# Three elementwise additions of a hybrid encoder kernel made by accumulating DMA transfers

## The chip, the cores and the metric

The kernel runs on one core of a Trainium2 chip. A core has a matrix engine (PE, with its weight loads as PEld), a vector engine (DVE), an activation engine (ACT), a general engine (POOL) and a queue engine (SP), which work side by side and wait for each other by semaphores; 16 DMA engines move data between memory and the core. DMAs are issued from the queues of SP, ACT and POOL. The metric is the device time of one execution in microseconds (us), the median of several; less is better.

## The reference

Two layers over 1040 positions (16 meta tokens ahead of 1024) of width 1024. Each layer has a mixer (a gated delta rule in both directions with 4 heads of 128, beside a short gated convolution) and a SwiGLU feed-forward part, each with an RMS norm ahead of it and added to the residual. Cut to what matters:

```python
def rmsnorm(x, w):
    y = xf * lax.rsqrt(jnp.mean(xf * xf, axis=-1, keepdims=True) + RMS_EPS)
    return y * w

def chunk_gated_delta_rule(q, k, v, g, beta):
    G = jnp.cumsum(g, axis=-1)
    incl = jnp.tril(jnp.ones((CHUNK, CHUNK), dtype=bool))
    decay_mat = jnp.exp(jnp.where(incl, G[..., :, None] - G[..., None, :], -jnp.inf))
    M = jnp.where(strict, jnp.einsum('bnhid,bnhjd->bnhij', kb, k) * decay_mat, 0.0)
    ...                     # triangular solves with I + M, then a scan over the chunks
def swiglu(h, w_gate_up, w_down):
    gate, up = jnp.split(h @ w_gate_up, 2, axis=-1)
    return (jax.nn.silu(gate) * up) @ w_down

for l in range(DEPTH):
    h = h + hybrid_mixer(rmsnorm(h, norm1_w[l]), ...)
    h = h + swiglu(rmsnorm(h, norm2_w[l]), w_gate_up[l], w_down[l])
h = rmsnorm(h, final_norm_w)
```

## The kernel before

Everything lies with channels on the 128 partitions and positions along the row. Matrix products in full precision are made of three passes: weights and inputs are split into a high and a low part (`whi`, `wlo`; `a`, `b` and others), and each tile of 128 channels takes high times high, high times low and low times high (L156 to L158 in `dense`, L1064 to L1066 in `prod`, L1430 to L1432 for the last product). A weight tile is loaded by SP into a `raw` or `ck2` buffer, ACT copies its high part (L129, L1046) and POOL, in some stretches DVE, subtracts for the low part (L130, L1047).

The program is written in Python as a list of instructions, and a planner, which simulates the times of instructions and transfers, draws up each engine's order from priorities and from what it reckons to be ready. On the chip every engine and every queue then goes through its own list strictly in order: an instruction that waits holds all behind it. Buffers with one tag are shared in turn; a new use waits until the old one is over. `after` and `at_prio` write some orders by hand.

A layer goes through these stages. Input projection: tiles of keys (`seq` 4 to 7), queries, values, gates and the convolution's channels. When the keys are there, `normalise` sends their lengths through memory on POOL's queue (`rnd`, L415, and `bc`, L418) and DVE multiplies (L419). `chunk_p` then makes, for each of nine chunks and two directions `d`, the decay matrix: row sums `gd` are loaded to all partitions into one of eight buffers `ptm` (L459, on ACT's queue), DVE adds a mask `off` of 0 and 1e30 (L460), ACT takes the exponential (L462), the result is stored (`dtd`, L463) and DVE multiplies it with the keys' products (L465). `sub_start` reuses the buffers of `ptm`: ACT copies the diagonal blocks (L521), DVE transposes them (L523), `substitute` inverts them on DVE (L533, L535), and `invert` finishes on PE (L544 transposes, L560 first product). For the first chunk, `meta` does small operations on POOL (L478, L479). A scan over the chunks follows (loads at L783 to L789).

Output projection: `out_part(z, m)` makes eight tiles `m` for each of two halves `z` of the positions; DVE adds them to the residual (L909), ACT squares them into `sq`, of which there are two buffers with the tag `c` (L953), and the squares are added to the running sum `ss` (in the profile `rstd`) by DVE, or by POOL for the even tiles of the second half (L954). `finish_bc` makes the norm's factors from the sums (L206 to L214). Beside it DVE and ACT prepare the inputs `T` of the feed-forward part (L177, L968 to L1005).

Feed-forward part: gate and up together are a two by two product of blocks done with seven products instead of eight. For each tile `f` of 22 the weights A11, A12, A21, A22 are loaded, and DVE forms sums and differences of them: `s1t` = A21 + A22 (L1288), `s2t` (L1289, L1292), A11 - A21 (L1293). `w_op` splits each. `NE` = 4: for the first four tiles the products with A11 and A12 are made ahead, under the end of the output projection. The tag `ck2` has five buffers, each `f` takes four of them. The down projection follows in the same way (`w_unit`, `t_pair`).

The lines that the change touches, outside the two functions:

```python
        off = sb.tile([128, 2, 128], F32, tag="off", name=nm("off"))
        dma(off.rearrange("p a b -> p (a b)"), cst_d[:, C_NF:C_NF + 256])          # L325
        ...
            s1t, s2t = raw4("ck2"), raw4("ck2")
            ...
            tt(out=s1t, in0=A21, in1=A22, op=ALU.add)                             # L1288
```

Of the kernel before, what the change touches and what calls it, by code (L numbers as in the profile page):

```python
# [7 lines left out]
F32 = mybir.dt.float32  # L8
# [3 lines left out]
ALU = mybir.AluOpType  # L12
# [6 lines left out]
H = 4  # L19
# [23 lines left out]
def trunk(ctx: ExitStack, tc: tile.TileContext, xT, w_in, w_ba, w_out, w_gu, w_dn,  # L43
          par_d, alog_d, dtb_d, cst_d, eye_d, out):
    nc = tc.nc
    sb = ctx.enter_context(tc.tile_pool(name="sb", bufs=1))
# [5 lines left out]
    def nm(p):  # L52
        cnt[0] += 1
        return f"{p}_{cnt[0]}"
# [220 lines left out]
    dma(alog, alog_d.partition_broadcast(128))  # L275
    dma(dtb, dtb_d.partition_broadcast(128))

    hsrc = xT
    for l in range(DEPTH):
        last = l == DEPTH - 1  # L280
# [39 lines left out]
        hd = dram.tile([KT, 128, L], F32, name=nm("hd"))  # L320
        m0d = dram.tile([2, 2, 4, 16, 16], F32, name=nm("m0d"))
        rsd = [dram.tile([4, 260], F32, name=nm("rsd")) for _ in range(2)]

        off = sb.tile([128, 2, 128], F32, tag="off", name=nm("off"))
        dma(off.rearrange("p a b -> p (a b)"), cst_d[:, C_NF:C_NF + 256])  # L325


        gt = big("P0")
# [117 lines left out]
        def chunk_p(c):  # L446

            if not Pd:
                Pd.extend(sb.tile([128, 4 * L], F32, tag=f"P{d}", name=nm("P")) for d in range(2))
                Pv.extend(p[:, 0:4096].rearrange("p (q i) -> p q i", i=128) for p in Pd)  # L450
                p_ = sb.tile([128, 4 * L], F32, tag=Y[0][2], name=nm("ptm"))
                ptm.extend(p_[:, 512 * i:512 * i + 512].rearrange("p (h i) -> p h i", h=4) for i in range(8))
            n, s0 = span(c)
            kk = bank("b").rearrange("p (h i) -> p h i", h=4)
            for h in range(H):
                mm(kk[0:n, h, 0:n], KTt[:, h, s0:s0 + n], KTt[:, h, s0:s0 + n], start=True, stop=True)
            for d in (dirs0 if c == 0 else (0, 1)):
                gr = ptm[(2 * c + d) % 8]
                adma(gr[0:n, :, 0:n], gd[36 * d + 4 * c:36 * d + 4 * c + 4, 0:n].partition_broadcast(n))  # L459
                tt(out=gr[0:n, :, 0:n], in0=gr[0:n, :, 0:n], in1=off[0:n, d, 0:n].unsqueeze(1).to_broadcast([n, 4, n]), op=ALU.add)  # L460
                for h in range(H):
                    act(out=gr[0:n, h, 0:n], in_=gr[0:n, h, 0:n], func=AF.Exp, scale=-1.0, bias=nGb[0:n, d, c, h:h + 1])  # L462
                adma(dtd[c, d].rearrange("p (h i) -> p h i", h=4)[0:n, :, 0:n], gr[0:n, :, 0:n])  # L463
                dst = P0[d] if c == 0 else Pv[d][:, 4 * c - 4:4 * c, :]
                tt(out=dst, in0=kk[0:n, :, 0:n], in1=gr[0:n, :, 0:n], op=ALU.mult)  # L465
                if c == 0:

                    def meta():
                        mt = t2k("mt").rearrange("p a b -> p (a b)")[0:4].rearrange("p (w a b) -> p w a b", w=2, a=16)
                        Wm, Zm = mt[:, 0], mt[:, 1]  # L470
                        Tm = t2k("mt").rearrange("p a b -> p (a b)")[0:4, 0:256].rearrange("p (a b) -> p a b", a=16)
                        dma(m0d[d, 0].rearrange("h j i -> j h i"), P0[d])
                        dma(Wm, m0d[d, 0])
                        dma(Zm, eye_d[0:4, :, :][:, 0:16, 0:16])
                        for s in (range(15, 0, -1) if d == 0 else range(0, 15)):
                            r0, r1, a0, a1 = (0, s, s, 16) if d == 0 else (s + 1, 16, 0, s + 1)
                            sh = [4, r1 - r0, a1 - a0]
                            ptt(out=Tm[:, r0:r1, a0:a1], in0=Wm[:, r0:r1, s:s + 1].to_broadcast(sh), in1=Zm[:, s:s + 1, a0:a1].to_broadcast(sh), op=ALU.mult)  # L478
                            ptt(out=Zm[:, r0:r1, a0:a1], in0=Zm[:, r0:r1, a0:a1], in1=Tm[:, r0:r1, a0:a1], op=ALU.subtract)  # L479
                        dma(m0d[d, 1], Zm)  # L480
                        dma(P0[d], m0d[d, 1].rearrange("h j i -> j h i"))

                    meta()
# [461 lines left out]
        def out_part(z, m):  # L945
            dense(wload(w_out[l, m, :, 0:4, :], 4), os_, hcut[z], add_h(m), pwide)

            v, sv = half(hr[m][:, o0:L], z), half(ss[:, o0:L], z)
            if m == 0:
                act(out=sv, in_=v, func=AF.Square)  # L950
            else:
                sq = c4k("sq")[:, 0:NB].rearrange("p (g e) -> p g e", g=2)
                act(out=sq, in_=v, func=AF.Square)  # L953
                (ptt if z == 1 and m % 2 == 0 else tt)(out=sv, in0=sv, in1=sq, op=ALU.add)  # L954
            for (n0, n1) in hcut[z]:
                dma(hd[m][:, n0:n1], hr[m][:, n0:n1])

# [320 lines left out]
        for f in range(FT):  # L1278
            A11, A12, A21, A22 = raw4("raw"), raw4("raw"), raw4("ck2"), raw4("ck2")
            dma(A11, w_gu[l, f, 0, :, 0:4, :])  # L1280
            dma(A21, w_gu[l, f, 1, :, 0:4, :])
            dma(A22, w_gu[l, f, 1, :, 4:8, :])
            dma(A12, w_gu[l, f, 0, :, 4:8, :])
            s1t, s2t = raw4("ck2"), raw4("ck2")
            W = {}
            if f >= NE:
                W["A11"] = w_op(A11)
            tt(out=s1t, in0=A21, in1=A22, op=ALU.add)  # L1288
            tt(out=s2t, in0=s1t, in1=A11, op=ALU.subtract)  # L1289
            W["S1"] = w_op(s1t)  # L1290
            W["S2"] = w_op(s2t)
# [281 lines left out]
```

## Time and profile before

| | |
|---|---|
| median of 3 runs | 2578.45 us (2576.64 to 2578.76) |
| profiled execution | 2583.93 us, span 2582.2 us |
| granted PE clock, mean | 0.993 |
| busy, share of the span | PE 97%, DVE 64%, POOL 44%, ACT 41% |
| DMA | 360.04 MB, mean 139 GB/s |
| POOL's DMA queue | 2176 packets, 4.36 MB |

The span runs from the first to the last instruction of the profiled execution. A row of a group reads: line, engine, operation, out<-in, shapes and count, then busy time and mean time of one in ns, then the idle time of that engine just before these instructions and what ended it. Rows in order of time begin with the start and the duration in us, and a bracket gives the idle time before. Rows of stretches give the busy time of each engine with its count of instructions, then the PE clock, the busy share of the DMA engines and GB/s. A row of waits gives the waiting engine and line, the releaser, the total in us, the count and the longest.

### The profile page before, as it was taken

The numbers are of one execution on the slowest core, as the hardware profiler recorded it, in microseconds if no ns is written. First come the engines' busy times: TensorE is split into PE (matmuls) and PEld (weight loads), VectorE is DVE, ScalarE is ACT, GpSimd is POOL, SyncE is SP. The second block draws the span as 40 slices with busy tenths as digits, with TensorE's granted clock in tenths as the row PEclk, the third lists the DMA queues.
The fourth block names the chain that finished last, engine by engine and source line by source line (L and its number), as shares of the span: only waits on it lengthen the run. The fifth ranks groups of instructions, "written<-read, shape, count | busy, mean of one in ns | idle before, by whom it ended". The sixth has DMA issues, their size and how long they took to land.

```text
span 2582.2 us, 45315 instructions
## 1 busy us (share of the span) xinstructions
PE 2501.5 (97%) x17508; PEld 2285.0 (88%) x17508; DVE 1651.3 (64%) x2461; ACT 1046.1 (41%) x1945; POOL 1139.5 (44%) x869
## 2 busy tenths in 40 slices
PE   8999999999999999999999989999999999999998
PEld 6888999998999999999998978999877787887877
DVE  4678523648766666778556885235597776768664
ACT  5574332435233333444445733324452333334444
POOL 2041212325666666655420202212467676675662
PEclk9999999999999999999999989999999999999999
DMA  3458365524432222574323682556343322227641
GB/s 124 127 173 266 109 192 167 193 71 131 137 108 87 88 82 82 189 236 139 95 95 121 198 261 92 152 176 208 102 131 123 121 90 88 90 90 263 194 122 66
DMA packets 213764, 360.04 MB, mean 139 GB/s; under 512 B 25460, under 2 KB 87868, under 8 KB 213548
## 3 DMA queue, kind: packets, MB, share of 16 engines
q1 hardware_dynamic: 180300, 310.17, 37.0%
q10 hardware_dynamic: 31072, 42.61, 5.3%
q0 software_dynamic: 2176, 4.36, 0.6%
q8 instruction: 137, 2.24, 0.4%
q14 instruction: 79, 0.65, 0.1%
HBM read 266.60 MB, written 90.46 MB: 138 GB/s over the span
## 4 chain that ended last, share of the span: by engine, by line
PE 52%; DVE 10%; DMA 4%; issue 3%; POOL 2%; ACT 1%; SPq 0%; ACTq 0%; DVEq 0%; POOLq 0%
PE pacc L156 5%; PE pacc L158 5%; PE pacc L157 5%; PE pacc L1064 3%; PE pacc L1066 3%; PE pacc L1065 3%; PE pb L1064 2%; PE pb L1065 2%; PE pb L1066 2%; PE pf L1064 2%; PE pf L1066 2%; PE pf L1065 2%; PE pacc L1432 1%; PE pacc L1430 1%; PE pacc L1431 1%
## 5 line engine op out<-in xcount | busy, mean ns | idle before, releaser
L130 POOL TENSOR_TENSOR wlo<-raw,whi 128x512 fp32r<-128x512 f32 x132 | 177.4, 1345 | 767.0 <-ACT whi L129 670.2
L156 PE MATMUL pacc<-a,whi 128*128 128x346 f32 (+1 forms) x808 | 264.4, 330 | 12.2 <-ACT whi L129 8.8
L158 PE MATMUL pacc<-a,wlo 128*128 128x346 f32 (+1 forms) x808 | 264.0, 329 | 1.9 <-DVE wlo L130 1.2
L156 PE MATMUL pacc<-b,whi 128*128 128x346 f32 (+2 forms) x672 | 235.0, 351 | 0.0
L158 PE MATMUL pacc<-b,wlo 128*128 128x346 f32 (+2 forms) x672 | 233.8, 349 | 0.0
L157 PE MATMUL pacc<-a,whi 128*128 128x346 f32 (+1 forms) x688 | 225.6, 328 | 0.3 <-DVE a L905 0.3
L129 ACT ACTIVATE whi<-raw 128x512 fp32r<-128x512 f32 x168 | 105.2, 628 | 248.0 <-PE pacc L157 164.7
L157 PE MATMUL pacc<-b,whi 128*128 128x346 f32 (+2 forms) x580 | 201.1, 348 | 0.3 <-DVE b L905 0.3
L156 PEld LDWEIGHTS pacc<-a,whi 128*128 128x128 f32 x808 | 153.4, 191 | 17.0 <-ACT whi L129 10.9
L1047 POOL TENSOR_TENSOR wlo<-rw,whi 128x512 fp32r<-128x512 f32 x92 | 135.9, 1478 | 71.4 <-ACT whi L1046 70.0
L158 PEld LDWEIGHTS pacc<-a,wlo 128*128 128x128 f32 x808 | 153.6, 190 | 3.8 <-DVE wlo L130 1.6
L156 PEld LDWEIGHTS pacc<-b,whi 128*128 128x128 f32 x672 | 127.4, 190 | 11.3 <-issue 3.1
L158 PEld LDWEIGHTS pacc<-b,wlo 128*128 128x128 f32 x672 | 127.5, 190 | 9.2 <-issue 0.8
L1047 POOL TENSOR_TENSOR a<-rw,a 128x512 fp32r<-128x512 f32 x64 | 105.5, 1649 | 68.1 <-ACT a L1046 67.8
L157 PEld LDWEIGHTS pacc<-a,whi 128*128 128x128 f32 x688 | 130.8, 190 | 4.5 <-issue 3.3
L1047 POOL TENSOR_TENSOR b<-rw,b 128x512 fp32r<-128x512 f32 x64 | 92.4, 1446 | 81.9 <-ACT b L1046 49.2
L157 PEld LDWEIGHTS pacc<-b,whi 128*128 128x128 f32 x580 | 110.2, 190 | 7.6 <-DVE b L905 0.6
L1046 ACT ACTIVATE whi<-rw 128x512 fp32r<-128x512 f32 x92 | 57.8, 630 | 144.2 <-DVE rw L1292 87.3
L1293 DVE TENSOR_TENSOR rw<-raw,rw 128x512 f32<-128x512 f32 x44 | 100.5, 2284 | 1.2
L1288 DVE TENSOR_TENSOR rw<-rw,rw 128x512 f32<-128x512 f32 x44 | 67.4, 1531 | 50.0 <-POOL wlo L1047 34.9
L1047 POOL TENSOR_TENSOR wlo<-raw,whi 128x512 fp32r<-128x512 f32 x50 | 77.9, 1561 | 33.5 <-ACT whi L1046 33.4
L1046 ACT ACTIVATE b<-rw 128x512 fp32r<-128x512 f32 x64 | 40.2, 630 | 120.7 <-PE pacc L1065 32.9
(970 smaller groups left out, 8429.2 us busy)
## 6 DMA issues: line engine op xcount, KB each, us to landing
raw<-in_w_in SPq DMA_DIRECT2D x112, 256.0 KB
raw<-in_w_gu SPq DMA_DIRECT2D x104, 256.0 KB
rw<-in_w_gu SPq DMA_DIRECT2D x88, 256.0 KB
rw<-in_w_dn SPq DMA_DIRECT2D x94, 192.0 KB
rec<-aqd SPq DMA_DIRECT2D x62, 256.0 KB
rec<-vkd SPq DMA_DIRECT2D x61, 256.0 KB
raw<-in_w_out SPq DMA_DIRECT2D x48, 256.0 KB
b<-ad SPq DMA_DIRECT2D x45, 260.0 KB
```

Of the source, the lines that this page charges most:

```text
L129: act(out=hi, in_=raw[:, 0:kk, :], func=AF.Copy)
L130: (tt if lov[0] else ptt)(out=lo, in0=raw[:, 0:kk, :], in1=hi.bitcast(F32), op=ALU.subtract)
L156: mm(ps[:, :n], wh, xh[:, n0:n1], start=(k == 0), stop=False)
L157: mm(ps[:, :n], wh, xl[:, n0:n1], start=False, stop=False)
L158: mm(ps[:, :n], wl, xh[:, n0:n1], start=False, stop=(k == K - 1))
L1046: act(out=hi, in_=src, func=AF.Copy)
L1047: ptt(out=lo, in0=src, in1=hi.bitcast(F32), op=ALU.subtract)
L1064: mm(ps[:, :CW], w[0][:, k, :], th[:, cs], start=first and k == 0, stop=False, skip_group_check=True)
L1065: mm(ps[:, :CW], w[0][:, k, :], tl[:, cs], start=False, stop=False, skip_group_check=True)
L1066: mm(ps[:, :CW], w[1][:, k, :], th[:, cs], start=False, stop=stop and k == nk - 1, skip_group_check=True)
L1288: tt(out=s1t, in0=A21, in1=A22, op=ALU.add)
L1293: tt(out=A21, in0=A11, in1=A21, op=ALU.subtract)
```

## The change

Three additions are taken from DVE (and POOL) and made by DMA transfers that add what they bring to what lies in their destination. Such transfers are issued from POOL's queue (`qdma` with `accum_op`).

The masks: instead of the tile `off` on the core, a tensor `offd` in memory is built once, the two masks repeated for four heads, by four copies on ACT's queue. For each chunk and direction SP loads the mask into the buffer `gr`, and POOL's transfer adds the row sums to it; the load on ACT's queue and the addition L460 go. The second norm's sums: each square `sq` is added to the sum by a transfer from buffer to buffer, instead of L954 on DVE or POOL. The weight sums A21 + A22 of the first four gate/up tiles: SP loads A21 a second time, into `s1t`, and POOL's transfer adds A22 from memory; for the other 18 tiles DVE adds as before. The buffers of `s1t` and `s2t` are taken in the order shown.

```diff
@@ trunk, ahead of the loop over the layers
+    offd = dram.tile([128, 2, 4, 128], F32, name=nm("offd"))
+    for h in range(H):
+        adma(offd[:, :, h, :], cst_d[:, C_NF:C_NF + 256].rearrange("p (a b) -> p a b", a=2))
@@ the layer's tiles
-        off = sb.tile([128, 2, 128], F32, tag="off", name=nm("off"))
-        dma(off.rearrange("p a b -> p (a b)"), cst_d[:, C_NF:C_NF + 256])
@@ chunk_p
-                adma(gr[0:n, :, 0:n], gd[36 * d + 4 * c:36 * d + 4 * c + 4, 0:n].partition_broadcast(n))
-                tt(out=gr[0:n, :, 0:n], in0=gr[0:n, :, 0:n], in1=off[0:n, d, 0:n].unsqueeze(1).to_broadcast([n, 4, n]), op=ALU.add)
+                dma(gr[0:n, :, 0:n], offd[0:n, d, :, 0:n])
+                qdma(gr[0:n, :, 0:n], gd[36 * d + 4 * c:36 * d + 4 * c + 4, 0:n].partition_broadcast(n), accum_op=ALU.add)
@@ out_part
-                (ptt if z == 1 and m % 2 == 0 else tt)(out=sv, in0=sv, in1=sq, op=ALU.add)
+                qdma(sv, sq, accum_op=ALU.add)
@@ the gate/up tiles
             dma(A22, w_gu[l, f, 1, :, 4:8, :])
+            if f < NE:
+                s1t = raw4("ck2")
+                dma(s1t, w_gu[l, f, 1, :, 0:4, :])
+                qdma(s1t, w_gu[l, f, 1, :, 4:8, :], accum_op=ALU.add)
             dma(A12, w_gu[l, f, 0, :, 4:8, :])
-            s1t, s2t = raw4("ck2"), raw4("ck2")
+            if f >= NE:
+                s1t = raw4("ck2")
+            s2t = raw4("ck2")
             W = {}
             if f >= NE:
                 W["A11"] = w_op(A11)
-            tt(out=s1t, in0=A21, in1=A22, op=ALU.add)
+            if f >= NE:
+                tt(out=s1t, in0=A21, in1=A22, op=ALU.add)
```

## The prediction

> **What bounds the kernel now.** I read the head of the page and its chain first, then the busy time by stretches around the changed lines, then waits and the order of time on single engines.
>
> ```profile
> span 2582.2 us, 45315 instructions
> PE 2501.5 (97%) x17508; PEld 2285.0 (88%) x17508; DVE 1651.3 (64%) x2461; ACT 1046.1 (41%) x1945; POOL 1139.5 (44%) x869
> PE 52%; DVE 10%; DMA 4%; issue 3%; POOL 2%; ACT 1%; SPq 0%; ACTq 0%; DVEq 0%; POOLq 0%
> q0 software_dynamic: 2176, 4.36, 0.6%
> ```
>
> PE has work in 97% of the span: all its idle time is 2582.2 - 2501.5 = 80.7 us, and that is the most that any relief of another engine could bring. The change takes work from DVE, which is second on the chain with 10%. The last row is POOL's DMA queue, the only one that the new transfers can use: so far 4.36 MB in the whole run.
>
> ```profile
> core 0: us, PE busy (x) PEld busy (x) DVE busy (x) ACT busy (x) POOL busy (x), PEclk, DMA share, GB/s
> 90.00:125.00 35.00, 32.15 (x207) 29.78 (x205) 22.85 (x32) 24.85 (x53) 4.66 (x8) 1.00 0.60 184
> 125.00:160.00 35.00, 31.84 (x228) 29.25 (x228) 25.75 (x39) 27.17 (x57) 21.74 (x60) 1.00 0.72 225
> 160.00:235.00 75.00, 70.56 (x689) 66.81 (x687) 61.39 (x129) 35.42 (x44) 9.02 (x14) 1.00 0.58 186
> 570.00:610.00 40.00, 40.00 (x337) 40.00 (x336) 30.13 (x51) 22.47 (x37) 20.28 (x15) 1.00 0.55 170
> 610.00:625.00 15.00, 9.97 (x66) 9.38 (x66) 15.00 (x18) 8.30 (x14) 9.18 (x6) 0.89 0.41 124
> 625.00:660.00 35.00, 32.86 (x268) 31.43 (x267) 28.13 (x29) 18.42 (x34) 20.23 (x14) 1.00 0.39 125
> 660.00:735.00 75.00, 69.69 (x570) 68.54 (x568) 55.17 (x77) 19.88 (x32) 45.50 (x27) 1.00 0.40 128
> ```
>
> These are the changed places in the first layer; the second repeats them. In 90 to 160 the masks are added: PE loses 2.9 and 3.2 us, with DVE far from full and the DMA engines already at 0.60 and 0.72. In 570 to 610 the second norm's sums run under the output projection: PE loses nothing. In 610 to 625 DVE is full and PE loses 5.0 us: a backlog on DVE. From 625 on come the gate/up tiles.
>
> **The change part by part.** Masks. What goes:
>
> ```profile
> L460 DVE TENSOR_TENSOR ptm<-ptm,off 128x512 f32<-128x512 f32 (+1 forms) x35 | 22.8, 661 | 20.5 <-DMA ptm<-gd 20.3
> 142.43 0.33 ACTq L459 DMA_DIRECT2D ptm<-gd  x1
> 146.33 0.69 DVE L460 TENSOR_TENSOR ptm<-ptm,off 128x512 f32<-128x512 f32 x1 [0.82 <-DMA ptm<-gd]
> 161.33 8.55 ACT L521 ACTIVATE b<-P 32x1024 f32<-32x1024 f32 x8 [1.89 <-DMA dtd<-ptm]
> PE pf L560 <- DVE a L544: 2.6, 1, 2.6
> ```
>
> 35 additions, 22.8 us of DVE, are removed. But DVE stood idle 20.3 us waiting for their rows to land, so they hardly held anyone. In their place stand a mask load on SP's queue and an accumulating row load on POOL's, which POOL may issue only when the mask has landed. For the first eight tiles the mask can land early, since their buffers are free. For the later ones, which reuse the buffers, two landings follow each other: 142.43 to 146.33 is 3.9 us for one, and POOL's issue (0.53 us, row below) is added and the 0.69 us of DVE are saved: +3.7 us; with a landing of 6.0 us, +5.8 us. The last of these tiles gates the copies of L521 (they wait for the store of that tile, and DVE has nothing to do meanwhile), these gate the substitution, and PE already waits for its result (L560 on L544, 2.6 us). If the planned order fits other PE work in between, it costs nothing; if not, the whole delay. I take 3 us a layer, 6 us. Below nothing: 91 to 125 holds evacuations that come late behind DVE, and 2.9 us a layer lost there is the most to be gained, so the bounds are -6 and +12 us.
>
> Behind the new POOL issues stand the key lengths:
>
> ```profile
> 98.69 2.49 POOL L415 DMA_DIRECT2D rnd<-b3f  x4 [16.38 <-DVE b3f L413]
> 104.18 1.19 POOL L418 DMA_DIRECT2D bc<-rnd  x2 [3.00 <-DMA rnd<-b3f]
> L418 POOL DMA_DIRECT2D bc<-rnd x8: 527/536/568, 104.2 to 1411.2; - x8
> DMA to landing us min/median/max: 3.9/6.0/10.3
> L783 SPq DMA_DIRECT2D rec<-vkd x35: 319/325/2010, 334.1 to 1807.2; - x35
> PE pa L427 <- DVE a L419: 2.5, 2, 2.3
> ```
>
> POOL was idle 16.38 us before them, so eight issues of 0.54 us (4.3 us) are hidden. Their transfers are not: 2 MB stand ahead of the lengths in the same queue, and PE waits for the normalised keys already (2.5 us). I take 2 us a layer, 4 us; bounds 0 and 10. POOL's small operations for the first chunk come between the accumulations, but only the scan, whose first load goes out at 334.1 us, needs them. The four copies that build the repeated mask at the start cost about four issues on ACT's queue, 4 x 0.33 = 1.3 us beside the first loads; I take 0.5 us.
>
> Second norm's sums. What goes:
>
> ```profile
> L954 DVE TENSOR_TENSOR rstd<-rstd,sq 128x520 f32<-128x520 f32 (+1 forms) x22 | 19.5, 888 | 1.9 <-ACT sq L953 1.9
> L954 POOL TENSOR_TENSOR rstd<-rstd,sq x6: 1313/1744/1774, 601.6 to 1901.7; 128x520 f32<-128x520 f32 x3, 128x512 f32<-128x512 f32 x3
> 579.87 0.72 DVE L954 TENSOR_TENSOR rstd<-rstd,sq 128x520 f32<-128x520 f32 x1
> 582.76 0.70 DVE L954 TENSOR_TENSOR rstd<-rstd,sq 128x520 f32<-128x520 f32 x1
> 607.20 0.70 DVE L954 TENSOR_TENSOR rstd<-rstd,sq 128x520 f32<-128x520 f32 x1 [0.16 <-ACT sq L953]
> 617.62 1.43 DVE L954 TENSOR_TENSOR rstd<-rstd,sq 128x520 f32<-128x520 f32 x1
> 627.23 0.69 DVE L954 TENSOR_TENSOR rstd<-rstd,sq 128x520 f32<-128x520 f32 x1
> ```
>
> Only the last three lie in the backlog: 0.70 + 1.43 + 0.69 = 2.8 us a layer, against 5.0 us that PE lost there. I count 2 us a layer as gained, -4 us; the bound is the whole 2.8, -6 us. The others ran beside a full PE and bring nothing.
>
> What comes is a chain. Seven sums a half, fourteen a layer, each adding to what the last one left, so POOL must see each land before it issues the next, and its `wlo` splits, which PE needs for every tile, wait behind it. Tiles follow each other every 582.76 - 579.87 = 2.89 us. No accumulating transfer is in this trace. The nearest link is POOL's own pair of the lengths: 0.56 us of issue and 3.00 us until it landed, 3.6 us, for a small transfer; with 0.5 us for 260 KB and for reading the destination, an estimate between that row and the 3.9 us in which the quickest of twice the size landed, 4.1 us. The ends are 2.9 us and below, where nothing is lost, and 0.54 + 6.0 = 6.5 us. At 4.1 us a layer lags 14 x (4.1 - 2.89) = 16.9 us; two tiles of weights prepared ahead take 5.8 us of it, 11 us are left, and I count 6, since the second half's links run on beside the early gate/up products and the planner may put splits first: +12 us; at 6.5 us in full, 14 x 3.6 - 5.8 = 45 us a layer, +90 us. ACT's squares too wait for one of two buffers, which now stay in use until a transfer lands.
>
> On the price of a link the Trainium skill, "DMA: Bandwidth & Descriptors", section "Anatomy of one DMA — SWDGE (gpsimd) path", fits about 2.0 us plus bytes over 436 GB/s for a transfer issued from GpSimd; an estimate from it for 266 KB is 2.6 us, and by it the chain would keep up and this term be -4 instead of +8 us. The 6.0 us median above for 520 KB is well over what the page's fit gives for it, 3.2 us, so I stay with the rows.
>
> First gate/up sums:
>
> ```profile
> L1288 DVE TENSOR_TENSOR rw<-rw,rw 128x512 f32<-128x512 f32 x44 | 67.4, 1531 | 50.0 <-POOL wlo L1047 34.9
> 649.54 0.69 DVE L1288 TENSOR_TENSOR rw<-rw,rw 128x512 f32<-128x512 f32 x1 [3.75 <-POOL wlo L1047]
> 661.18 0.42 DVE L1312 TENSOR_TENSOR a<-pacc,a 128x260 f32<-128x260 f32 x1
> 650.26 0.63 ACT L1046 ACTIVATE a<-rw 128x512 fp32r<-128x512 f32 x1 [2.74 <-DVE rw L1288]
> 643.94 1.30 POOL L1047 TENSOR_TENSOR wlo<-rw,whi 128x512 fp32r<-128x512 f32 x1
> PE pacc L1064 <- DVE a L1330: 6.0, 12, 1.5
> ```
>
> Eight of 44 additions go, 8 x 1.53 = 12 us of DVE, in 625 to 735 where DVE is 83 of 110 us busy. Before, the addition began the moment its buffer came free and took 0.69 us. Now from that moment a load on SP (3.9 us), POOL's issue (0.5) and an accumulation (3.6) follow: 8.0 us, so the sum is ready at 657.5 instead of 650.2, and ACT and POOL have still to split it, 0.63 + 1.30 us: 659.5. The product that uses it is evacuated at 661.18; its twelve matmuls of 69.69 / 570 = 0.12 us begin 1.5 us before that, at 659.7: the slack is used up. SP, waiting for the buffer, holds the next weight loads, and POOL, waiting for the load, the splits. I take 1.5 us a layer, +3 us; bounds -4 (a third of the 12 us reaches PE) and +14 us (8.0 - 0.7, exposed once a layer).
>
> Sum: 0.5 + 6 + 4 + 8 + 3 = 21.5 us. The profiled execution took 2583.9 us, 1.7 over its span and 5.5 over the median; 2583.9 + 21.5 = 2605.4, and on the median's scale 2578.5 + 21.5 = 2600 us.
>
> **The rivals.** *The transfers keep up* (faster). If an accumulating link lands in under 2.89 us, the sums lose nothing, the masks' two landings are fitted in by the order, and the relief of DVE is all that is left: -6 for the backlog, -4 at the gate/up tiles, 0 at the masks: 2568 us. For it speaks that PE waits for DVE in the gate/up tiles (6.0 us on the evacuations of L1330); against it the 3.00 us of the short link, and POOL's DMAs landing in 6.0 us. It decides at 2.89 us a link. Chance 0.2.
>
> *POOL becomes the bound of the output projection* (much slower). With 6.5 us a link in strict order the sums cost 90 - 4, with the other 13.5 about 100 us: 2678 us. For it: the row of 6.0 us, and DMA engines at 0.55 already there. Against it: the splits can be put ahead. Chance 0.15. It has a second support in how DVE and POOL hold each other up:
>
> ```profile
> 598.90 1.52 DVE L1005 TENSOR_SCALAR a<-a,par 128x520 f32<-128x520 f32 x1
> 602.67 0.50 DVE L1005 TENSOR_SCALAR a<-a,par 128x520 f32<-128x520 f32 x1 [0.91 <-DMA hd<-a]
> ```
>
> The same instruction takes 0.50 us alone and 1.52 us beside a split on POOL; a link that met each of the four of a layer would lose 4 x 1.0 us. The Trainium skill, "SBUF — State Buffer", section "SBUF: two separate sides", says that such an instruction of DVE keeps GpSimd from writing the descriptors of its own DMAs, so that these look slow; the 6.0 us above may hold some of that, and no row here tells it apart.
>
> *All is hidden* (within 0.2%, 5 us either way, which is about what a measurement here can tell): the costs of some 10 us cancel the gain of 10 us: 2578 us. Chance 0.08.
>
> **How the numbers follow.** The forecast, a moderate loss, keeps 0.57. Slower is 0.57 + 0.15 = 0.72, same 0.08, faster 0.2. The range takes in half of the faster rival and nearly half of the much slower one: 2566 to 2675 us, about a tenth left out at each end. The forecast's own range is 2585 to 2640.
>
> **What would show it.** In the profile after, the landing of the accumulating transfers in the sums (4.1 us) and POOL's waits for them; PE idle in the 40 us of the output projection, where it had none; the backlog on DVE behind it shorter by 3 us; the copies of L521 about 4 us later after the keys. I am wrong if PE stays full in the output projection and the DVE backlog is the only thing that moved, or if a link takes over 6 us.

## The result and the profile after

The changed kernel takes 2637.82 us (median of 4 runs, 2634.90 to 2640.69) against 2578.61 us for the kernel before on the same chip (2576.64 to 2579.59): ratio 1.0228, 95% interval 1.0210 to 1.0246, or 59 us slower. Forecast were 21.5 us and 2600 us: the direction was right, but the loss is well over twice the one forecast, at the very end of the forecast's own range (2585 to 2640 us).

The head of the page of after (lines of a queue end with packets, MB and share):

```profile
span 2637.3 us, 45403 instructions
PE 2518.3 (95%) x17508; PEld 2300.8 (87%) x17508; DVE 1629.7 (62%) x2396; ACT 1053.0 (40%) x1949; POOL 1179.2 (45%) x934
q0 software_dynamic: 14000, 22.26, 4.7%
PE 39%; DMA 5%; DVE 4%; issue 2%; ACT 1%; POOL 1%; ACTq 0%; DVEq 0%; SPq 0%; POOLq 0%
```

DVE's busy time fell by 21.6 us and its share of the chain from 10% to 4%. But the masks' and the sums' additions alone had taken 22.8 + 19.5 = 42.3 us of DVE: the rest of its work has become longer, by instructions shown below. Nothing of the relief came back as time. PE's idle time rose from 80.7 to 2637.3 - 2518.3 = 119.0 us, +38.3. And the same 17508 matmuls were busy 16.8 us longer. Together these are the 55.1 us by which the span grew. The second part goes with the granted clock, 0.983 in the mean where it was 0.993, as the stretches show:

```profile
90.00:125.00 35.00, 31.87 (x206) 29.68 (x205) 19.87 (x27) 27.37 (x52) 10.66 (x16) 1.00 0.72 195
125.00:160.00 35.00, 31.29 (x213) 27.43 (x212) 16.54 (x23) 22.59 (x49) 21.96 (x63) 0.90 0.98 267
570.00:610.00 40.00, 36.60 (x299) 35.77 (x298) 22.81 (x32) 17.86 (x29) 21.97 (x20) 1.00 0.72 187
610.00:650.00 40.00, 28.89 (x200) 27.70 (x198) 38.69 (x41) 21.64 (x35) 20.16 (x16) 0.87 0.63 147
650.00:680.00 30.00, 26.57 (x207) 25.82 (x208) 14.30 (x18) 10.67 (x22) 19.55 (x14) 0.94 0.52 153
680.00:740.00 60.00, 49.54 (x375) 47.63 (x373) 39.65 (x51) 12.72 (x20) 35.13 (x21) 0.94 0.39 118
```

The columns are those of before. In the output projection (570 to 610) PE was full and now loses 3.4 us; in the next 40 us it loses 11.1, and DVE is full in them (38.69 of 40; in the same 40 us of before it was busy for 34.73): the backlog that the change was to shorten is longer. From 610 on the granted clock is 0.87 to 0.94.

Part of that backlog comes from the links, which bring instructions of DVE into step with POOL's splits. One DVE instruction of the output projection, before and after:

```profile
L177 DVE SCALAR_TENSOR_TENSOR a<-a,par,a x4: 746/748/752, 583.4 to 592.0; 128x520 fp32r<-128x520 f32 x4
L177 DVE SCALAR_TENSOR_TENSOR a<-a,par,a x4: 1864/1872/1897, 586.9 to 599.4; 128x520 fp32r<-128x520 f32 x4
```

In after each of the four, and each of their like in the second layer, begins 0.2 to 0.3 us behind a split on POOL (586.90 and 586.66 us for the first), and takes 1.87 us in place of 0.75. In every kernel below but the one with the sums alone it starts elsewhere and takes 0.74 to 0.76 us. With the scalings of L1007 (L1005 before), 14.9 us for eight in place of 6.8, this makes 17 us of DVE in the two layers.

The longest waits of PE say who holds PE (engine and line, releaser, us in total, times, longest):

```profile
PE pacc L156 <- ACT whi L129: 15.3, 4, 7.1
PE pa L429 <- ACT kt L431: 7.5, 3, 5.1
PE pacc L158 <- POOL wlo L130: 6.0, 8, 1.5
PE pb L1066 <- ACT whi L1048: 5.2, 1, 5.2
PE pf L158 <- POOL wlo L130: 4.2, 4, 2.0
```

PE waits for the weights' high and low parts, from ACT and POOL, which wait in their turn (the first row was 8.8 us in two waits before; its longest, 7.1 us, lies ahead of the first matmul and was 6.0). In the wait of 5.2 us PE stands from 628.2 to 633.3 us, and from there to 638.0 the granted clock is 0.50. This agrees with the Trainium skill, "TensorE: Matmul & The Clock Gate", section "What's actually happening", by which an idle stretch of about 3.4 us halves the clock. Of the seventeen falls of the clock ahead of the end of this trace nine come with PE idle for 2.8 to 5.2 us, some of them thus for less than the page's time; beside the others there is no single gap of that length.

Where this happens is seen from SP's stores: the first row of the residual, and the fifth gate/up tile. Before:

```profile
568.51 0.33 SPq L956 DMA_DIRECT2D hd<-a  x1
742.12 0.33 SPq L1357 DMA_DIRECT2D ad<-a  x1
```

After:

```profile
570.54 0.33 SPq L958 DMA_DIRECT2D hd<-a  x1
770.38 0.33 SPq L1366 DMA_DIRECT2D ad<-a  x1
```

From one to the other 173.6 us became 199.8, +26.2 in the first layer (by the same two stores of the second layer +23.7). So 50 of the 55 us of the two profiled executions lie in the output projection and the first gate/up tiles, where two of the three parts of the change are. The 5 us that this leaves to the masks are too few: ten kernels below that leave the masks as they were make the first of these stores at 561 to 566 us, so the profiled execution of before was some microseconds slow ahead of it.

POOL's order of time in after shows the chain of links, with a split (now and then two) behind each:

```profile
581.08 0.86 POOL L956 DMA_DIRECT2D rstd<-sq  x1 [1.88 <-DMA rstd<-sq]
582.02 1.29 POOL L130 TENSOR_TENSOR wlo<-raw,whi 128x512 fp32r<-128x512 f32 x1
586.05 0.86 POOL L956 DMA_DIRECT2D rstd<-sq  x1 [2.74 <-PE pacc L158]
586.66 1.58 POOL L130 TENSOR_TENSOR wlo<-raw,whi 128x512 fp32r<-128x512 f32 x1
...
594.62 0.86 POOL L956 DMA_DIRECT2D rstd<-sq  x1 [2.46 <-DMA rstd<-sq]
595.23 1.55 POOL L130 TENSOR_TENSOR wlo<-raw,whi 128x512 fp32r<-128x512 f32 x1
...
636.85 1.19 POOL L956 DMA_DIRECT2D rstd<-sq  x1 [1.91 <-ACT a L1101]
```

The first of the fourteen links begins at 576.27, the last at 636.85: 60.58 / 13 = 4.66 us a link, where a tile took 2.89 us. The line's own view gives issue and landing:

```profile
L956 POOL DMA_DIRECT2D rstd<-sq x28: 855/1040/1228, 576.3 to 1949.1; - x28
  DMA rstd<-sq: 12.0, 7
...
  ACT sq L955: 7.9, 4
DMA to landing us min/median/max: 3.3/3.9/5.2
```

In seven waits POOL stood 12.0 us for a landing, and in four ACT stood 7.9 us for a buffer that a square still occupied. The other waits ahead of a link are put down to other engines, and some of them may be landings too.

### The profile page after: what moved, and what is told of

It reads as the page before. It is cut to its first block, busy times and chain, and to the rows that moved or that the text cites. A ratio compares the mean times of both kernels' runs of the same rounds, so it can differ in the third digit from the quotient of the medians.

```text
span 2637.3 us, 45403 instructions
## 1 busy us (share of the span) xinstructions
PE 2518.3 (95%) x17508; PEld 2300.8 (87%) x17508; DVE 1629.7 (62%) x2396; ACT 1053.0 (40%) x1949; POOL 1179.2 (45%) x934
## 4 chain that ended last, share of the span: by engine, by line
PE 39%; DMA 5%; DVE 4%; issue 2%; ACT 1%; POOL 1%; ACTq 0%; DVEq 0%; SPq 0%; POOLq 0%
PE pacc L156 5%; PE pacc L158 5%; PE pacc L157 4%; PE pacc L1068 2%; PE pacc L1066 2%; PE pacc L1067 2%; PE pb L1067 1%; PE pb L1066 1%; PE pb L1068 1%; PE pf L1066 1%; PE pf L1068 1%; PE pf L1067 1%; DMA ptm<-gd 1%; PE pacc L1441 1%; PE pacc L1440 1%
## 5 line engine op out<-in xcount | busy, mean ns | idle before, releaser
L130 POOL TENSOR_TENSOR wlo<-raw,whi 128x512 fp32r<-128x512 f32 x132 | 182.5, 1389 | 697.5 <-ACT whi L129 630.5
L1049 POOL TENSOR_TENSOR wlo<-raw,whi 128x512 fp32r<-128x512 f32 x50 | 79.4, 1594 | 20.4 <-ACT whi L1048 20.0
L300 DVE TENSOR_TENSOR a<-pacc,rstd 128x346 f32<-128x346 f32 (+2 forms) x59 | 32.6, 552 | 85.7 <-PE pacc L158 85.7
```

The lines of the kernel that those rows point to most:

```text
L130: (tt if lov[0] else ptt)(out=lo, in0=raw[:, 0:kk, :], in1=hi.bitcast(F32), op=ALU.subtract)
L300: tt(out=t[:, n0:n1], in0=ps, in1=rstd[:, n0:n1], op=ALU.mult)
L1049: ptt(out=lo, in0=src, in1=hi.bitcast(F32), op=ALU.subtract)
```

## The experiments

My theory (A at first): each of the three parts costs by itself, the sums most, since a chain of links is slower than the tiles and POOL goes through its list in order. Rivals: the adding itself, the traffic, POOL's issue time, and later the planner's new order. The ratios are to the kernel before on the same chip, us are differences of the medians:

| kernel | ratio, 95% interval | us |
|---|---|---|
| sums alone | 1.0121, 1.0094 to 1.0149 | +34.1 |
| masks alone | 1.0068, 1.0048 to 1.0089 | +18.7 |
| gate/up sums alone | 1.0062, 1.0043 to 1.0080 | +16.7 |
| sums, two chains | 1.0050, 1.0032 to 1.0068 | +11.8 |
| masks, no adding | 1.0032, 1.0019 to 1.0046 | +8.3 |
| row sums on POOL's queue | 1.0017, 1.0000 to 1.0033 | +5.1 |
| gate/up, one transfer | 1.0020, 1.0008 to 1.0032 | +4.1 |
| sums, plain on ACT's queue | 1.0011, 0.9998 to 1.0024 | +2.6 |
| odd sums by transfer | 1.0059, 1.0046 to 1.0072 | +15.4 |
| second half on POOL | 1.0055, 1.0043 to 1.0067 | +15.0 |
| sums, splits on DVE | 1.0078, 1.0065 to 1.0092 | +21.9 |
| masks, late tiles only | 1.0045, 1.0033 to 1.0057 | +11.9 |
| POOL adds tiles 1, 3, 5 | 1.0052, 1.0038 to 1.0065 | +12.0 |
| second half on DVE | 1.0004, 0.9995 to 1.0014 | +1.2 |

**Each part alone.** Three kernels with one part of the change each; their edits are the three parts of the diff above.

> Only the second norm's sums are made by accumulating transfers; masks and weight sums as before. Theory A (the chain on POOL): a sum waits for the one before it to land and the weight splits wait behind it, so tiles of the output projection come every 4.7 us instead of 2.89 us: 25 to 30 us in all, 2604 to 2609 us. Rival C (the weight sums of the gate/up tiles hold most of the loss): under 12 us, below 2591 us.

> Only the masks are added by accumulating transfers. From the shift of the stages in the changed kernel: 2 us in the first layer and 7 in the second, 9 us, 2588 us. Rival (the masks' two landings in a row hold most of the loss, and the later stages only pass it on): 20 us or more, from 2599 us.

> Only the first four weight sums of each layer's gate/up tiles are made by accumulating transfers. Theory A: a load, POOL's issue and an accumulation in a row (8 to 9 us) stand in place of an addition of 0.7 us, seen about twice a layer: 12 to 18 us, 2591 to 2597 us. If the chain of the norm's sums caused all of that stage's loss: within 4 us of the kernel before.

+34.1, +18.7 and +16.7 us, 69.5 in sum against 59.2 together: the parts nearly add up, as they would if they hardly touched each other. The gate/up sums lie in theory A's range, the sums above it, and the masks between the 9 us expected and the rival's 20. Every one of the prediction's terms was too small: the sums had +8, the masks +10, the gate/up sums +3.

**Sums on two chains.** The tiles add in turn to two rows, which PE joins in `finish_bc` with a second matmul of ones (in parts; the edit is against the kernel with the sums alone):

```diff
+        ss2 = row(X[1] + "f")
-            v, sv = half(hr[m][:, o0:L], z), half(ss[:, o0:L], z)
+            v, sv = half(hr[m][:, o0:L], z), half((ss, ss2)[m % 2][:, o0:L], z)
-            if m == 0:
+            if m < 2:
...
-                qdma(sv, sq, accum_op=ALU.add)
+                qdma(half((ss, ss2)[m % 2][:, o0:L], z), sq, accum_op=ALU.add)
-        finish_bc(ss, o0, L, rsd[0])
+        finish_bc(ss, o0, L, rsd[0], ss2=ss2)
```

> As e1, but even and odd tiles add to two different sums, which the ones-matmuls of the norm join at the end: a transfer waits for the one before last, and the tile rate of 2.89 us needs a link of at most 5.8 us. Theory A (waiting for the last landing): the output projection runs at its old pace, within 5 us of the kernel before, 2574 to 2584 us. Rival B (POOL's issue time of 1.0 us and the load on the DMA engines cost it, not the wait): nearly as slow as e1, still 15 us or more over the kernel before.

+11.8 us, between the two theories: of the 34.1 us, 22 go away although 24 of the 28 transfers are left and POOL still issues each. The intervals of the two ratios lie apart, and PE's order is nearly the same in both (more on that below). That the single chain costs most of the sums' part is shown. The line's view of this kernel no longer has a wait for a landing; POOL waits for the squares, that is for work to be done (the transfers of one of the two rows, the waits of both):

```profile
L957 POOL DMA_DIRECT2D rstd<-sq x12: 837/1074/1646, 570.3 to 1900.0; - x12
  ACT sq L956: 16.1, 8
DMA to landing us min/median/max: 3.9/4.8/5.9
```

**Sums, splits on DVE.** One chain again, but nothing that PE needs stands behind it on POOL:

```diff
+            lov[0] = True
+            ws = wload(w_out[l, m, :, 0:4, :], 4)
+            lov[0] = False
-            dense(wload(w_out[l, m, :, 0:4, :], 4), os_, hcut[z], add_h(m), pwide)
+            dense(ws, os_, hcut[z], add_h(m), pwide)
```

> The one chain of sums by transfers (+34.1 us) as it was, but the low parts of the output projection's weights are subtracted on DVE instead of POOL: the splits stand no longer behind the links in POOL's queue. The chain itself stays as long. Theory A, the splits behind the links cost most of it: back to +5 to +15 us, with PE almost full in 560 to 602. Theory B, it is the chain's length, the norm that waits for the last link at the end of each half: +25 us or more. DVE gets some 30 splits of 0.7 us a layer in place of its sums, which may cost up to 8 us of its own.

+21.9 us, between the two theories. POOL's order of time shows what remains:

```profile
570.21 0.96 POOL L957 DMA_DIRECT2D rstd<-sq  x1 [22.49 <-ACT sq L956]
575.00 0.86 POOL L957 DMA_DIRECT2D rstd<-sq  x1 [3.83 <-issue]
...
629.94 1.19 POOL L957 DMA_DIRECT2D rstd<-sq  x1 [1.98 <-ACT P L971]
```

With none of the output projection's splits on POOL (those of the gate/up tiles stand between the last four), the fourteen links still take (629.94 - 570.21) / 13 = 4.6 us each. So the splits behind the links are part of the matter, some 12 us of the 34 and more if they cost DVE something in turn. To these belongs what they did to DVE: here the instruction of L177 takes 0.76 us again. The chain itself is as long as it was, and that its end is what is left of the cost is likely, but the sixteen splits a layer that DVE makes now (0.69 us each; thirty were expected) are in the 21.9 us too.

**Sums as plain copies on ACT's queue.** Two rows as above, and

```diff
-                qdma(half((ss, ss2)[m % 2][:, o0:L], z), sq, accum_op=ALU.add)
+                adma(half((ss, ss2)[m % 2][:, o0:L], z), sq)
```

> Second norm's sums on two alternating rows (+11.8 us as they were), but the transfers leave POOL: plain copies on ACT's queue, nothing is added, so the norm's sums are left out of the output. The transfers, their bytes and the buffers they hold stay. Theory A, the rest of 11.8 us is POOL's time at the links (issue 0.84 to 1.2 us each and waiting, in front of the splits): at most +4 us, and PE full from 570 to 610. Theory B, it is the traffic (the DMA engines at 0.78 there, 0.55 before) or the two buffers of the squares held until a transfer lands: +8 us or more.

+2.6 us, as theory A's range said: the same bytes (366.39 and 366.38 MB in all), with the squares' buffers held until they land (3.9 us median), cost nothing that can be told. Traffic and buffers are out as causes of the 11.8 us; the adding and the place in POOL's queue went away together.

**Odd sums by transfer, and the second half on POOL.** The first edit is against the two chains, the second against the kernel before.

```diff
-                qdma(half((ss, ss2)[m % 2][:, o0:L], z), sq, accum_op=ALU.add)
+                if m % 2 == 1:
+                    qdma(sv, sq, accum_op=ALU.add)
+                else:
+                    tt(out=sv, in0=sv, in1=sq, op=ALU.add)
```

```diff
-                (ptt if z == 1 and m % 2 == 0 else tt)(out=sv, in0=sv, in1=sq, op=ALU.add)
+                (ptt if z == 1 else tt)(out=sv, in0=sv, in1=sq, op=ALU.add)
```

> Second norm's sums: only the odd tiles go by accumulating transfers, into a row of their own (three links a half instead of seven); the even tiles are added by DVE in both halves, none by POOL's own additions; the two rows are joined in the matmuls with ones. A link of 4.66 us has two tiles' time, 5.8 us. Theory A, the links cost because they are slower than one tile's pace and POOL waits: now they keep up, POOL hardly waits for landings, -2 to +4 us. Theory B, each accumulating transfer costs by itself (issue, traffic, buffer) about what is left of the two alternating chains, 11.8 us for 24 links: 12 links, +5 to +7 us.

> No transfers: the kernel before, with all seven sums of the second half on POOL instead of the even ones, so DVE keeps none in its backlog. Theory A, the backlog on DVE is what PE loses there and 2.8 us a layer of sums lie in it: -2 to -5 us. Theory B, the four more sums of 1.74 us on POOL delay its splits of the first gate/up tiles by as much as DVE gains: -1 to +4 us.

+15.4 and +15.0 us: all four expectations missed. Half of the transfers cost no less than all of them on two chains, and four sums moved between two engines, with no transfer at all, cost as much. Neither POOL's load (in the second half, three links of 1.2 us in place of three sums of 1.7 in the first kernel, four sums more in the second) nor the links explain both.

**A null edit, and its opposite.** What both have in common is that the order of the first gate/up tiles is planned anew. Two kernels without transfers were to test that, one with POOL's sums a tile away from their old places, one with all sums on DVE:

```diff
-                (ptt if z == 1 and m % 2 == 0 else tt)(out=sv, in0=sv, in1=sq, op=ALU.add)
+                (ptt if z == 1 and m in (1, 3, 5) else tt)(out=sv, in0=sv, in1=sq, op=ALU.add)
```

```diff
-                (ptt if z == 1 and m % 2 == 0 else tt)(out=sv, in0=sv, in1=sq, op=ALU.add)
+                tt(out=sv, in0=sv, in1=sq, op=ALU.add)
```

> A null change for the sums: no transfers, the kernel before, but in the second half POOL adds the squares of tiles 1, 3 and 5 instead of 2, 4 and 6, so that DVE and POOL do as many sums as before, each one tile away from its old place, and the order is planned anew. Theory A, the places and not the planning cost: -3 to +3 us. Theory B, any change of these sums makes the planner draw up another order of the first gate/up tiles, and that order by itself costs some us: +6 to +15 us, lost between the first and the fifth gate/up tile as in the two kernels before this that moved sums without a long chain.

> No transfers: the kernel before, with all sums of the second half on DVE, so POOL has three fewer (1.74 us each, 5.2 us a layer) and DVE three more (0.7 to 1.5 us). Theory A, POOL's time ahead of the first splits sets the end there (four sums more on POOL cost 15 us): -4 to -12 us, a version better than before. Theory B, DVE's backlog sets it: +3 to +8 us. Theory C, any new order loses some us there: +6 to +15 us, and the loss lies behind the sums, between the first and the fifth gate/up tile.

+12.0 us for an edit that leaves every engine the same number of sums, and +1.2 us for one that moves three of them. The null edit's sums in its own profile:

```profile
L954 DVE TENSOR_TENSOR rstd<-rstd,sq x22: 677/718/1785, 569.6 to 1908.7; 128x520 f32<-128x520 f32 x11, 128x512 f32<-128x512 f32 x11
L954 POOL TENSOR_TENSOR rstd<-rstd,sq x6: 1368/1747/2260, 593.4 to 1894.9; 128x520 f32<-128x520 f32 x3, 128x512 f32<-128x512 f32 x3
```

22 and 6, as before. From the first store of the residual to the fifth gate/up tile this kernel takes 179.6 us against 173.6 (its rows are 564.64 and 744.21). Theory B of the first run held by its range; in the second all three missed. Counted from the traces, 1769 of the 17368 matmuls of PE (without those with the matrix of ones) stand elsewhere in the order than before, against 497 in the kernel that cost nothing, which looks as if the new order were the cost.

The plain copies on ACT's queue speak against that: 1830 matmuls stand elsewhere there, and they cost 2.6 us. From their order the kernel with one chain differs in only 55 matmuls, the one with two chains in 115, the one with the second half on POOL in 31, and POOL's splits come in the same order in all four. So what these four differ in, 34.1, 11.8, 15.0 and 2.6 us, is hardly the planned order: some 22 us are the one chain against two, some 9 the adding from POOL's queue against plain copies on ACT's, and some 12 the sums that DVE and POOL make themselves. What a new order costs by itself is not shown. The copies also relieve DVE and POOL of the sums, which may hide some of its cost, and the null edit moved the places of POOL's sums along with the order. So 12 us without any change of load are on record, their cause is open, and single differences of that size stay open too where the order differs, as that of the 12 us of the splits does (676 matmuls).

**Masks: without adding, and on POOL's queue alone.** The first edit is against the kernel with the masks alone, the second against the kernel before.

```diff
-                qdma(gr[0:n, :, 0:n], gd[36 * d + 4 * c:36 * d + 4 * c + 4, 0:n].partition_broadcast(n), accum_op=ALU.add)
+                qdma(gr[0:n, :, 0:n], gd[36 * d + 4 * c:36 * d + 4 * c + 4, 0:n].partition_broadcast(n))
...
-                    act(out=gr[0:n, h, 0:n], in_=gr[0:n, h, 0:n], func=AF.Exp, scale=-1.0, bias=nGb[0:n, d, c, h:h + 1])
+                    act(out=gr[0:n, h, 0:n], in_=gr[0:n, h, 0:n], func=AF.Exp, scale=-0.0, bias=epsc[0:n, 0:1])
```

```diff
-                adma(gr[0:n, :, 0:n], gd[36 * d + 4 * c:36 * d + 4 * c + 4, 0:n].partition_broadcast(n))
+                qdma(gr[0:n, :, 0:n], gd[36 * d + 4 * c:36 * d + 4 * c + 4, 0:n].partition_broadcast(n))
```

> Masks alone, as in the run with only the masks (+18.7 us), but POOL's transfer of the row sums overwrites the mask instead of adding to it, and the exponential is taken with a factor of zero so that it stays finite: the mask and the decay itself are left out of the output. Both landings in series, POOL's queue and its issues stay; only the adding in the transfer is gone. Theory A, the order costs it (two landings in series, POOL held between them, eight tiles ahead of the key lengths): +14 to +20 us, as with adding. Theory B, adding transfers are slow by themselves (landing 8.1 us median against 3.9 to 6.0): +4 to +9 us and a landing back at some 4 us.

> The kernel before with one word changed: the row sums are loaded on POOL's queue instead of ACT's, without adding; the mask stays on the core and DVE adds it. One landing a tile, but the transfers stand in POOL's queue ahead of the key lengths. Theory A, the two landings in series are what costs with the masks: 0 to +5 us. Theory B, the place in POOL's queue ahead of the key lengths costs most of it (their pair was 4.3 us later in the run with only the masks): +8 to +15 us, and the pair starts at about 108 us instead of 104.

+8.3 us and +5.1 us (the second's interval begins at no change). I had held the two landings in series for the cause, and in the first run theory B's range held: the same two transfers in series without the adding cost less than half. PE and DVE go through exactly the same order in this kernel and in the one with the adding, so the 10 us between them are not the plan's. In the second, +5.1 us is far from theory B's 8 to 15: a place in POOL's queue ahead of the key lengths costs little. The lines of the row sums in the two kernels, first with the adding, then without:

```profile
L463 POOL DMA_DIRECT2D ptm<-gd x35: 837/897/3219, 91.5 to 1451.1; - x35
  ACT ptm L465: 21.5, 13
DMA to landing us min/median/max: 2.2/8.1/13.1
```

```profile
L463 POOL DMA_DIRECT2D ptm<-gd x35: 536/558/741, 90.6 to 1439.8; - x35
  ACT ptm L465: 13.0, 9
DMA to landing us min/median/max: 1.8/5.9/8.4
```

Issue 0.90 us against 0.56, landing 8.1 against 5.9 us (not back at the 4 us that theory B expected). The key lengths stand behind eight of these; POOL's order of time with the adding:

```profile
100.95 0.55 POOL L418 DMA_DIRECT2D rnd<-b3f  x1 [0.56 <-DMA ptm<-gd]
108.49 1.10 POOL L421 DMA_DIRECT2D bc<-rnd  x2 [6.99 <-DMA rnd<-b3f]
```

and without:

```profile
103.46 1.10 POOL L421 DMA_DIRECT2D bc<-rnd  x2 [3.71 <-DMA rnd<-b3f]
```

POOL waits 6.99 or 3.71 us for the lengths to land, with 3.00 in the kernel before and 2.13 in the one with the row sums on POOL's queue: what delays the keys is not eight transfers ahead of them but that they add. On this the Trainium skill, "Collectives: The Full Stack", section "Stop ④ — SDMA + CCE: where bytes move and the add happens", has the add "free in between" of reading two streams and writing one. It speaks of collectives, not of transfers that POOL issues into the core; here the rows differ by 0.34 us of issue and 2.2 us of landing, and the rows decide.

**Masks on the late tiles only.**

```diff
+                if c < 4:
+                    adma(gr[0:n, :, 0:n], gd[36 * d + 4 * c:36 * d + 4 * c + 4, 0:n].partition_broadcast(n))
+                    tt(out=gr[0:n, :, 0:n], in0=gr[0:n, :, 0:n], in1=off[0:n, d, 0:n].unsqueeze(1).to_broadcast([n, 4, n]), op=ALU.add)
+                else:
```

> Masks alone (+18.7 us), but the first eight tiles of a layer (chunks 0 to 3), whose accumulations stood on POOL ahead of the key lengths, go as before: load on ACT's queue, mask added by DVE. The other ten, in reused buffers, go by mask load and accumulating transfer. Theory A, the eight accumulations ahead of the key lengths cost about half (their pair was 4.3 us later a layer): +7 to +11 us, with the pair back at about 104 us. Theory B, the later tiles with their two landings in series and SP held by them cost nearly all: +14 us or more.

+11.9 us, just above A's range. The pair is back (POOL's order of time), and the late tiles still wait:

```profile
101.87 1.25 POOL L424 DMA_DIRECT2D bc<-rnd  x2 [2.36 <-DMA rnd<-b3f]
...
151.48 0.89 POOL L470 DMA_DIRECT2D ptm<-gd  x1 [4.30 <-DMA ptm<-offd]
154.73 0.59 POOL L470 DMA_DIRECT2D ptm<-gd  x1
```

So about 7 of the 18.7 us seem to come from the eight accumulations ahead of the keys, and the rest from the other tiles, whose last accumulation goes out at 154.7 us; the two kernels' orders differ (1138 matmuls), so this division is not shown. Before, the last addition was done at 148.3 (DVE's order of time):

```profile
147.61 0.69 DVE L460 TENSOR_TENSOR ptm<-ptm,off 128x512 f32<-128x512 f32 x1 [0.59 <-DMA ptm<-gd]
```

The DMA engines are at 0.99 from 125 to 160 in this kernel and at 0.98 in after, against 0.72 before; that this is what makes them late was not tried.

**Gate/up sums with one plain transfer.**

```diff
-                dma(s1t, w_gu[l, f, 1, :, 0:4, :])
-                qdma(s1t, w_gu[l, f, 1, :, 4:8, :], accum_op=ALU.add)
+                qdma(s1t, w_gu[l, f, 1, :, 4:8, :])
```

> Gate/up sums alone (+16.7 us as they were), but the sum is left out: one plain transfer of A22 from POOL's queue into the buffer, without the load of A21 ahead of it. So one landing (about 4 us) from the moment the buffer is free instead of two (8 us), and POOL waits for a free buffer instead of a landing. Theory A, the length of the chain load, issue, accumulation sets the cost: +2 to +8 us. Theory B, it is POOL's queue held up in front of the splits, whatever it waits for: +12 to +17 us.

+4.1 us, as theory A said. POOL still issues a transfer in front of the splits, so the length of the chain, which now has one landing and no adding, is what seems to cost. Who waited for the transfer, in the kernel with only the gate/up sums (L1286) and here (L1285):

```profile
  DVE rw L1296: 19.0, 3
  ACT a L1046: 11.6, 2
  ACT b L1046: 8.3, 1
```

```profile
  ACT a L1046: 3.5, 1
  DVE rw L1295: 2.6, 2
  ACT b L1046: 0.6, 1
```

38.9 us of waiting on DVE and ACT became 6.7. But the difference of 12.6 us is about what the null edit cost, and the two orders differ in 629 matmuls, so the size is not settled, only the waits are.

No kernel here beats the one before; the nearest, all sums of the second half on DVE, is even with it.

## Why the prediction was off

*Sums, +8 forecast, +34.1 measured.* The mechanism was right, a chain slower than the tiles, but three steps were sized wrong. First the price of a link: 4.1 us forecast, 4.66 measured, since issue took 0.86 to 1.2 us, where 0.56 were taken, and the landing 3.9 us, where 3.5 were taken. (The fit of the Trainium skill, "DMA: Bandwidth & Descriptors", section "Anatomy of one DMA — SWDGE (gpsimd) path", that the prediction cites gives 2.6 us; the landings of the 28 links are 3.3 to 5.2 us.) The half microsecond looks small, but the lag is the difference to 2.89: 14 x 0.56 = 7.8 us more a layer, 16 for both. Second the halving: "11 us are left, and I count 6, since the second half's links run on beside the early gate/up products and the planner may put splits first". Link and split alternate to the end of the row, and the total agrees with the whole lag: 5 us a layer, 10 for both. By the rule without the halving, 14 x (4.66 - 2.89) - 5.8 = 19 us a layer, 38 for both, near the 34; how the 34 divide among these steps is worked out and not measured. Third, the gain of 4 us on DVE's backlog did not come. What the prediction had named beside its second rival only, a link that makes DVE slower, came and went further: 1.0 us for each of four scalings a layer was named and 8.1 us were measured for all eight, and the eight of L177 took 9 us more.

*Masks, +10 forecast, +18.7 measured.* The step that failed is the landing: "+3.7 us" a late tile was taken from a landing of 3.9 us; with the adding the median was 8.1, and 5.9 without. For the key lengths 2 us a layer were taken; POOL's wait for them grew from 3.00 to 6.99 us with the masks alone and to 6.26 in after. The eight issues, 7.2 us and not 4.3, were still hidden: the lengths go out at 98.69 us before and with the masks alone. The copies of L521 began at 161.33 and begin at 165.16 in after, 3.8 us later, where 4 were forecast (ACT's order of time):

```profile
165.16 8.56 ACT L523 ACTIVATE b<-P 32x1024 f32<-32x1024 f32 x8 [0.65 <-DMA dtd<-ptm]
```

That the two agree so well is luck: in the ten kernels with the old masks these copies begin between 156.0 and 161.7 us, so the start in the profile of before is a late one.

*Gate/up sums, +3 forecast, +16.7 measured.* The chain of 8.0 us was about right (its landings are 4.4 and 4.1 us in after, the issue 0.9), and it came out too that the slack is used up. "I take 1.5 us a layer" is the step: the four tiles of a layer each have the chain, and its waits on DVE and ACT are long. The upper bound of 14 us counted it once a layer, and the measured loss is above it.

*What no term had.* The sum counted PE's idle time only. With the 38.3 us more of idle time came 16.8 us of slower matmuls. And every term took the order of before for granted; an edit that changes no load moved the time by 12 us, by its order or by the places of POOL's sums.

Of the signs named, PE's idle time in the output projection, the waits for the landings and the later copies came; the shorter backlog did not.

## What to carry to other kernels

A transfer that adds takes an instruction from a busy engine, but as a chain on one destination it has a pace, issue plus landing, and it must be faster than the loop that feeds it; if it isn't, split the destination first and count the whole lag, not half. Look at what stands behind it in the issuing queue and at what waits for the last link. Look also at which instructions of other engines the landing starts at the same moment. And before reading a few microseconds as the cost of an edit in a planned kernel, run a null edit at the same place, or compare with a kernel that the planner has put into the same order; the traces tell which do.

## What the runs showed that I had not expected

An adding transfer from core to core costs POOL 0.86 us to issue in the first half and 1.19 in the second; its plain ones took 0.53 to 0.56. In the landing the adding from core to core costs little: 4.8 us on two rows, against 3.9 for the plain copies on ACT's queue into two rows; on one chain it is 3.9 too. For the rows from memory it costs more, 8.1 against 5.9 us in the median (13.1 against 8.4 at most).
